# Strided attention on one core: outputs evicted into the place of their Q blocks, and stored four groups at a time

## The chip, the cores and the metric

The kernel runs on one core of one Trainium2 chip. A core has five engines that run their own instruction streams and meet at semaphores: TensorE (PE; its weight loads are listed as PEld), VectorE (DVE), ScalarE (ACT), GpSimd (POOL) and SyncE (SP), which here issues all the transfers. The transfers themselves are done by 16 DMA engines between the chip's memory (HBM) and the on-chip memory SBUF, which has 128 partitions.

The metric is the time of one execution on the device in microseconds (us). The profile is of one such execution, and its span runs from the first to the last instruction.

## The reference

Q, K and V have the shape (8, 12, 1024, 64) in float32. Every query of a head attends to the same 16 key positions, those at multiples of 64:

```python
attend_positions = np.arange(0, seq, stride)          # 0, 64, ..., 960
q = Q[:, :, i:i + 1, :].copy()
k = K[:, :, attend_positions, :].copy()
v = V[:, :, attend_positions, :].copy()
scores = np.einsum('bhqd,bhkd->bhqk', q, k) * scale   # scale = 1 / sqrt(64)
weights = np.exp(scores - np.max(scores, axis=-1, keepdims=True))
weights = weights / (np.sum(weights, axis=-1, keepdims=True) + 1e-10)
result[:, :, i, :] = np.einsum('bhqk,bhkd->bhqd', weights, v)[:, :, 0, :]
```

All of Q is read (96 heads of 256 KiB, 24 MiB), one row in 64 of K and of V (384 KiB each), and an output as large as Q is written.

## The kernel before, in words

The 96 heads are worked on in 24 groups (`NG`) of four heads (`HG`). A group is 1 MiB of Q and 1 MiB of output, 8 KiB in each of the 128 partitions. For group g these steps follow each other:

- `load(g)`: SP issues one transfer of the group's Q into the buffer `qn[g % QBUFS]`. There are 11 such buffers.
- `cast(g)`: POOL copies it to bfloat16 in `qb` (for the first three groups ACT does half).
- `transpose(g)`: DVE transposes it in blocks into `qt`.
- `scores(g)`: PE multiplies by the keys `k_t` into `sc`.
- `largest(g)`, `raise_(g)`, `sums(g)`: DVE takes the maximum and subtracts it, ACT takes the exponential into `ex`, DVE sums and takes the reciprocal.
- `weights(g)`: POOL multiplies `ex` by the reciprocal.
- `turn(g)`, `spread(g)`: PE transposes the weights into `tp`, ACT writes them into `wb`.
- `outputs(g, n)`: PE multiplies by the values `v_all` into the two halves of `o`.
- `evict(g, n)`: ACT copies each half from `o` into an output buffer in SBUF. There are 8 of these (`OBUFS`), in four tiles of two.
- `store(g, n)`: SP issues the transfer of n groups to HBM. Groups 0 to 13 are stored singly, 14 to 21 in pairs, 22 and 23 singly.

The order is written out by hand. Before the main loop K and V are read and spread into `k_t` and, over the first stages, into `v_all` by the small casts of `values`. The main loop goes over stages i; the list `ORDER` names each step with its lag, so that stage i works on the transpose of group i, the cast of i+1, the weights of i-2, the spread of i-3 and the evictions of i-4. Each engine takes its instructions in this order. PE runs a real loop of two stages per turn and counts on "gates", semaphores that the other engines raise; at the end dummy instructions raise them for stages that have no group any more.

SP's queue is ordered by `queue(g)`, the last step of a stage: after the evictions of group g it issues the load of group g+12, if there is one, and then the store, or, for pairs, the store after every second group. The first eleven loads stand in front of the main loop. A load waits for the cast that read its buffer; an eviction into a reused output buffer waits for the store that left it (`after=[stored[g - OBUFS]]`). The very last store is issued after the loop and does not wait for the older ones to land.

`Program.op` records each step with what it reads and writes, and `Program.plan` derives the waits from that; transfers have a "lane" of their own, whose semaphore counts their landing.

Of the kernel before, what the change touches and what calls it, by code (L numbers as in the profile page):

```python
# [168 lines left out]
def kernel(  # L169
# [8 lines left out]
    nc = tc.nc  # L178
# [25 lines left out]
    k_raw = late[:, 0 : NC * D].rearrange("p (n d) -> p n d", d=D)  # L204
    k_half = late[:, NC * D : 2 * NC * D].bitcast(BF16).rearrange("p (a n d) -> p a n d", a=2, d=D)
    k_bf, k_r = [k_half[:, i] for i in range(2)]
# [19 lines left out]

    prog = Program(nc, tc)
    op = prog.op
    stored = {}

    def load(g):
        n = 32
        op("SP", lambda: _copy(
            nc, qn[g % QBUFS],
            _ap_with(Q, [[HG * SD // n, n], [1, HG * SD // n]], g * HG * SD),
        ), writes=[f"qn{g % QBUFS}{h}" for h in range(2)], lane=f"q{g % QBUFS}")

    kv_src = [[stride * D, P], [2 * HG * SD, NC], [1, D]]

    def load_rows(name, tile_, src, lane):  # L240
        op("SP", lambda: nc.sync.dma_start(tile_, _ap_with(src, kv_src)),
           writes=[name], lane=lane)

    load_rows("k_raw", k_raw, K, f"out{OBUFS - 2}")
    load(0)
    load_rows("v_raw", v_raw, V, f"out{OBUFS - 1}")
    for g in range(1, QBUFS):
        load(g)

    op("POOL", lambda: nc.gpsimd.memset(identity, 0.0), writes=["identity"])  # L250
# [11 lines left out]
        op=ALU.max, axis=mybir.AxisListType.XY,  # L262
    ), reads=["identity"], writes=["sel"])
    op("POOL", lambda: nc.gpsimd.memset(v_all, 0.0),  # L264
       writes=[f"v{c}{a}{b}{m}" for c in range(2) for a in range(2) for b in range(2) for m in range(2)] + ["none"])

    def key_rows():
        op("ACT", lambda: nc.scalar.copy(k_bf, k_raw), reads=["k_raw"], writes=["k_bf"])  # L268
# [13 lines left out]
            )[:, h % 2],  # L282
        ), reads=["k_r"], writes=[f"k_t{c}{h}"])

    parts = (slice(0, 2), slice(2, NC))

    apart = []

    def values(c, a, b, m):
        src, dst, part = 32 * (2 * c + b), 32 * (2 * a + b), parts[m]  # L290
        op("POOL", lambda: nc.gpsimd.tensor_copy(  # L291
            out=v_all[dst : dst + 32, 3 + c + 2 * part.start : 3 + c + 2 * part.stop - 1 : 2, 2 * a + b],
            in_=v_raw[src : src + 32, part],
        ), reads=["v_raw"] + apart, writes=[f"v{c}{a}{b}{m}"])
        apart[:] = [f"v{c}{a}{b}{m}"]
# [1 line left out]
    half = 16 * D  # L297

    def cast(g, shared):
        q, b = qn[g % QBUFS], qb[g % 2]  # L300
        if shared:
            op("ACT", lambda: nc.scalar.copy(b[:, half:], q[:, half:]),  # L302
               reads=[f"qn{g % QBUFS}1"], writes=[f"qb{g % 2}1"])
            op("POOL", lambda: nc.gpsimd.tensor_copy(out=b[:, 0:half], in_=q[:, 0:half]),  # L304
               reads=[f"qn{g % QBUFS}0"], writes=[f"qb{g % 2}0"])
        else:
            op("POOL", lambda: nc.gpsimd.tensor_copy(out=b, in_=q),  # L307
               reads=[f"qn{g % QBUFS}{h}" for h in range(2)] + apart,
               writes=[f"qb{g % 2}{h}" for h in range(2)])
            apart[:] = [f"qb{g % 2}0"]  # L310

    def transpose(g):
        k_in = {0: "0", 1: "1"}.get(g)
        words = qt[g % 2].bitcast(I32)
        if g >= NG:
            op("DVE", lambda: nc.vector.memset(qt[g % 2][:, 0:2], 0.0), reads=["low"], writes=[f"qt{g % 2}"],
               gate="turned")
            return
        op("DVE", lambda: nc.vector.transpose(  # L319
            _ap_with(words, [words.ap[0], [1, 2], [D, 16], [2, 32]]), qb[g % 2].bitcast(I32),  # L320
        ), reads=[f"qb{g % 2}0", f"qb{g % 2}1"] + [f"k_t{k_in}{h}" for h in range(4) if k_in],
           writes=[f"qt{g % 2}"], gate="turned")
# [35 lines left out]
           reads=[f"total{g % 2}"], writes=[f"rec{g % 2}"])  # L358

    def weights(g):  # L360
        if g >= NG:
            op("POOL", lambda: nc.gpsimd.memset(wt[g % 2][:, 0:1, 0:2], 0.0), writes=[f"wt{g % 2}"], gate="weighted")
            return
        op("POOL", lambda: nc.gpsimd.tensor_tensor(  # L364
            out=wt[g % 2], in0=ex[g % 2],
            in1=rec[g % 2].unsqueeze(2).to_broadcast([P, 32, NK]), op=ALU.mult,
        ), reads=[f"ex{g % 2}", f"rec{g % 2}"] + [k for k in apart if k[0] == "v"], writes=[f"wt{g % 2}"], gate="weighted")

    def turn_products(g):
        for c in range(4):  # L370
# [29 lines left out]

    def outputs(g, n):
        op("PE", None, reads=[f"wb{g % 2}0", f"wb{g % 2}1"] + [
               f"v{g % 2}{a}{b}{int(g >= 4)}" if 0 <= g < NG else "none" for a in range(2) for b in range(2)
           ], writes=[f"o{n}"], gates=[(f"free{n}", g + 1)] if g >= 0 else [], looped=True)

    def evict(g, n):
        to = out_sb[g % OBUFS].rearrange("p b (c x) d -> p c b (x d)", c=4)
        half = slice(2 * n, 2 * n + 2)
        plain = g >= NG - 1 - 2 * n
        ready = [f"wb{(g + 1) % 2}0", f"wb{(g + 1) % 2}1"] * (n == 0)  # L410
        op("ACT", lambda: nc.scalar.copy(  # L411
            to[:, half], o_ps[:, half].rearrange("p c (b x) -> p c b x", b=2)
        ), reads=[f"o{n}"] + ready, writes=[f"out{g % OBUFS}.{n}"] + ["k_raw", "k_bf", "k_r"] * (g == OBUFS - RUN and not n),
           after=[stored[g - OBUFS]] if g >= OBUFS and not n else [],
           gate=None if plain else f"free{n}", last=g == NG - 1 and n == 1)

        if plain:
            free([f"out{g % OBUFS}.{n}"], n)
# [12 lines left out]
    def store(g, n):  # L431
        both = range(g, g + n)
        sent = op("SP", lambda: send(g, n), lane=f"out{g % OBUFS}",
                  reads=[f"out{i % OBUFS}.{n}" for i in both for n in range(2)])
        stored.update((i, sent) for i in both)

    def idle(i):
        scores(i)
# [24 lines left out]
    quadrants = [[(c, a, b, m) for c in range(2) for a in range(2) for b in range(2)] for m in range(2)]  # L463
    VALUES = {0: quadrants[0]}
    VALUES.update((i + 1, quadrants[1][2 * i : 2 * i + 2]) for i in range(4))

    DEPTH = 4
    turns = (NG + 4) // TURN
    ahead = 1

    def queue(g):
        for n in range(g + QBUFS + ahead if g else QBUFS, g + QBUFS + ahead + 1):
            if n < NG:
                load(n)
        if g < SINGLE or g == NG - 2:
            store(g, 1)
        elif g % RUN == RUN - 1 and g < NG - 1:
            store(g - RUN + 1, RUN)

    def at(i, stage, lag):  # L480
        g = i - lag
        if g in early.get(stage, ()):
            return
        if stage == "transpose" and 0 <= g < NG + 4:
            transpose(g)
        elif stage == "scores" and 0 <= g < NG + 4:
            scores(g)
        elif stage == "weights" and 0 <= g < NG + 2:
# [55 lines left out]
_INS = ['Q', 'K', 'V', 'stride']  # L544
# [31 lines left out]
```

## Time and profile before

| | |
|---|---|
| time, median of 3 runs | 129.38 us (129.22 to 129.51) |
| the profiled execution's own time | 128.91 us |
| its span | 126.7 us |
| busy: PE, DVE, ACT, POOL | 67.0, 86.4, 96.8, 81.8 us |
| moved by DMA | 51.16 MB, mean 404 GB/s |
| read from HBM, written to HBM | 25.95 MB, 25.17 MB |
| loads of Q | 24 of 1 MiB, median 15.6 us from issue to landing |
| stores | 16 of 1 MiB (14.4 us), 4 of 2 MiB (13.4 us) |

How to read the rows that follow: in a timeline a row has the start (us from the span's start), the duration, the engine, the line of the kernel, the operation and the tiles (output, then what it is made from), how many instructions were merged, and in brackets how long the engine had been idle and what ended that. "SPq" is SP's queue, where a row is the issue of a transfer and not the transfer. A row of DMA issues has what is moved, how many issues, KB of each and the median us from issue to landing. A row of the groups has line, engine, operation, shapes and count, then the sum of busy us, the mean ns of one, and the idle time before. A row of waits has who waited for whom, and us in total, times, longest. A row of the table of stretches has from:to, its length, the busy us and the number of instructions of PE, PEld, DVE, ACT and POOL, the granted clock of PE, the mean share of the DMA engines in use, and GB/s.

### The profile page before, as it was taken

Reading aid. Unit: us, or ns where it says so; the run is one execution under the profiler, and the core shown is the slowest. Engines: PE = TensorE matmul, PEld = TensorE weight load, DVE = VectorE, ACT = ScalarE, POOL = GpSimd, SP = SyncE. Lnnn points to the kernel's source line nnn. Section 1 sums busy time; section 2 is a strip of 40 time slices with the busy share of each in tenths; the row PEclk is TensorE's granted clock in tenths of the full one; section 3 lists DMA queues with packets and bytes.
Section 4 is the critical chain, followed back from the end, with each engine's and each line's share of the span. In section 5 each row is a group of like instructions: output and inputs, shape, how many; then the busy total and the mean of one; then the engine's idle time right before and its main releaser. Section 6 shows DMA issues by size and latency. Waiting matters only on the chain. (4 is left out here: it accounts for less than half of the span.)

```text
span 126.7 us, 2269 instructions
## 1 busy us (share of the span) xinstructions
PE 67.0 (53%) x784; PEld 48.7 (38%) x784; DVE 86.4 (68%) x129; ACT 96.8 (76%) x133; POOL 81.8 (65%) x73
## 2 busy tenths in 40 slices
PE   0003893055862666665885466474666658867000
PEld 0003571044642454443664344253554436635000
DVE  3614989565967789999999999999999955200000
ACT  4289614137977999999999999999999999996000
POOL 5982388999999977778877777887777123300000
PEclk9999999955599968998569999999689985699955
DMA  1997998989979899999999899899899999999980
GB/s 46 406 445 341 486 455 372 496 383 445 476 305 522 339 432 440 411 437 445 398 442 463 372 465 476 346 502 406 380 416 429 432 419 445 424 429 419 406 357 39
DMA packets 7141, 51.16 MB, mean 404 GB/s; under 512 B 3808, under 2 KB 3808, under 8 KB 3808
## 3 DMA queue, kind: packets, MB, share of 16 engines
q1 hardware_dynamic: 7136, 51.12, 96.5%
q14 instruction: 5, 0.04, 0.1%
HBM read 25.95 MB, written 25.17 MB: 403 GB/s over the span
## 5 line engine op out<-in xcount | busy, mean ns | idle before, releaser
L411 ACT COPY out_sb<-o 128x1024 f32<-128x1024 f32 x48 | 46.3, 1015 | 2.1
L307 POOL CAST qb<-qn 128x2048 bf16<-128x2048 f32 x21 | 39.7, 1889 | 0.1
L391 PE MATMUL o<-v_all,wb_all 128*128 x224 | 38.4, 313 | 2.2 <-ACTq L421 0.7
L364 POOL TENSOR_TENSOR wt_all<-ex,rec 128x512 bf16<-128x512 f32 x24 | 25.4, 1057 | 21.3 <-DVE rec L357 20.7
L383 ACT ACTIVATE wb_all<-tp,sel 128x512 bf16<-128x512 bf16 x48 | 30.4, 690 | 6.3 <-PE tp L371 6.2
L319 DVE STREAM_TRANSPOSE qt<-qb 128x1024 int32<-128x1024 int32 x24 | 29.8, 1240 | 6.3 <-ACT qb L302 3.3
L327 PE MATMUL sc<-k_t,qt 128*128 x448 | 23.4, 209 | 18.7 <-DVE qt L319 13.6
L327 PEld LDWEIGHTS sc<-k_t,qt 128*128 128x128 bf16 x448 | 20.1, 109 | 25.1 <-issue 23.3
L371 PE MATMUL tp<-identity,wt_all 128*128 128x128 bf16 x112 | 12.9, 249 | 29.0 <-POOL wt_all L364 28.5
L391 PEld LDWEIGHTS o<-v_all,wb_all 128*128 128x128 bf16 x224 | 22.6, 113 | 10.8 <-ACT out_sb L411 4.9
L354 DVE TENSOR_REDUCE total<-ex 128x32 f32<-128x512 f32 x24 | 16.3, 680 | 9.7 <-ACT ex L349 9.7
L349 ACT ACTIVATE ex<-low 128x512 f32<-128x512 f32 x24 | 15.4, 641 | 6.2 <-DVE low L344 6.2
L371 PEld LDWEIGHTS tp<-identity,wt_all 128*128 128x128 bf16 x112 | 7.5, 108 | 32.0 <-POOL wt_all L364 31.3
L344 DVE TENSOR_TENSOR low<-sc,top 128x512 f32<-128x512 f32 x24 | 16.6, 692 | 0.8
L341 DVE TENSOR_REDUCE top<-sc 128x32 f32<-128x512 f32 x24 | 15.2, 632 | 1.3 <-PE sc L327 1.3
L357 DVE RECIPROCAL rec<-total 128x32 f32<-128x32 f32 x24 | 8.5, 353 | 0.8
L291 POOL CAST v_all<-v_raw 32x128 bf16<-32x128 f32 (+1 forms) x16 | 8.0, 500 | 1.0
L264 POOL MEMSET v_all<- 128x7168 bf16 x1 | 6.1, 6071 | 0.0
L304 POOL CAST qb<-qn 128x1024 bf16<-128x1024 f32 x3 | 3.1, 1040 | 4.2 <-DMA qn<-in_Q_dram 4.2
L278 ACT COPY k_t<-out_sb 32x384 bf16<-32x384 bf16 x8 | 4.1, 508 | 0.7 <-DVE out_sb L269 0.6
L302 ACT CAST qb<-qn 128x1024 bf16<-128x1024 f32 x3 | 3.1, 1040 | 0.0
L268 ACT CAST out_sb<-out_sb 128x768 bf16<-128x768 f32 x1 | 0.8, 831 | 2.7 <-DMA out_sb<-in_K_dram 2.7
(14 smaller groups left out, 6.4 us busy)
## 6 DMA issues: line engine op xcount, KB each, us to landing
qn<-in_Q_dram SPq DMA_DIRECT2D x24, 1024.0 KB, 15.6
out_dram<-out_sb SPq DMA_DIRECT2D x16, 1024.0 KB, 14.4
out_dram<-out_sb SPq DMA_DIRECT2D x4, 2048.0 KB, 13.4
out_sb<-in_K_dram SPq DMA_DIRECT2D x1, 384.0 KB, 4.4
v_raw<-in_V_dram SPq DMA_DIRECT2D x1, 384.0 KB, 7.1
```

The source lines that it names most:

```text
L307: op("POOL", lambda: nc.gpsimd.tensor_copy(out=b, in_=q), reads=[f"qn{g % QBUFS}{h}" for h in range(2)] + apart, writes=[f"qb{g % 2}{h}" f ...
L319: op("DVE", lambda: nc.vector.transpose(_ap_with(words, [words.ap[0], [1, 2], [D, 16], [2, 32]]), qb[g % 2].bitcast(I32),), reads=[f"qb{g ...
L327: r = nc.tensor.matmul(sc_ps[g % 2][:, 64 * i : 64 * i + 64], lhsT=_ap_with(qt[g % 2], [qt[g % 2].ap[0], [2, P]], extra_offset=2 * P * i + f),
L341: op("DVE", lambda: nc.vector.tensor_reduce(out=m, in_=s, op=ALU.max, axis=mybir.AxisListType.X,), reads=[f"sc{g % 2}"], writes=[f"top{g % ...
L344: op("DVE", lambda: nc.vector.tensor_tensor(out=low, in0=s, in1=m.unsqueeze(2).to_broadcast([P, 32, NK]), op=ALU.subtract,), reads=[f"sc{g ...
L349: op("ACT", lambda: nc.scalar.activation(out=ex[g % 2], in_=low, func=AF.Exp, bias=0.0, scale=scale,), reads=["low"], writes=[f"ex{g % 2}"])
L354: op("DVE", lambda: nc.vector.tensor_reduce(out=total[g % 2], in_=ex[g % 2], op=ALU.add, axis=mybir.AxisListType.X,), reads=[f"ex{g % 2}"] ...
L364: op("POOL", lambda: nc.gpsimd.tensor_tensor(out=wt[g % 2], in0=ex[g % 2], in1=rec[g % 2].unsqueeze(2).to_broadcast([P, 32, NK]), op=ALU.mult,
L371: r = nc.tensor.transpose(tp_ps[g % 2][:, 2 * c : 2 * c + 2].rearrange("p a b -> p (a b)"), wt[g % 2][:, 8 * c : 8 * c + 8].rearrange("p t ...
L383: op("ACT", lambda a=a: nc.scalar.activation(out=wb[g % 2][:, :, 64 * a : 64 * a + 64], in_=tp_ps[g % 2], func=AF.Copy, scale=sel[:, a : a ...
L391: r = nc.tensor.matmul(_ap_with(o_ps, [o_ps.ap[0], [128, 2], [256, 2], [1, D]], extra_offset=512 * c + D * u,), lhsT=wb[g % 2][:, 2 * c + ...
L411: op("ACT", lambda: nc.scalar.copy(to[:, half], o_ps[:, half].rearrange("p c (b x) -> p c b x", b=2)), reads=[f"o{n}"] + ready, writes=[f" ...
```

## The change

Outputs get no buffers of their own any more. There are 16 buffers in four tiles of four (`quads`, `BUFS`, `RUN`), and each is first the place of a group's Q and then of the same group's output: `evict(g, n)` writes into `qn[g % BUFS]`, whose Q the cast has read long before. K's tiles, which lay in the last output tile, become tiles of their own.

Sixteen loads are issued ahead instead of eleven. A store takes one whole tile: four groups, 4 MiB, rows of 32 KiB per partition, each made of eight pieces of 4 KiB that go to eight places 512 KiB apart in HBM. There are six stores instead of twenty. The eight loads that are left are issued in two batches of four: 16 to 19 right behind the store of groups 4 to 7, when the store of 0 to 3 has landed, and 20 to 23 behind the store of groups 8 to 11, when that of 4 to 7 has landed. The last store, of groups 20 to 23, is the one issued after the loop.

Beside that, the values of the odd groups are cast in one piece each instead of two (`parts[1]`), so that there are 12 casts instead of 16; two of the four dummy steps of `transpose` go, and both dummy steps of `weights`, with the gates raised by several counts at once (`times`).

```diff
-    QBUFS = 11
-    OBUFS = 8
-    RUN = 2
-    SINGLE = 14
+    BUFS = 16
+    RUN = 4
...
-    qn = [sb.tile([P, 32 * D], FP32, name=f"qn{i}") for i in range(QBUFS)]
-    out_all = [sb.tile([P, RUN, 2, 16, D], FP32, name=f"out_sb{i}") for i in range(OBUFS // RUN)]
-    out_sb = [out_all[i // RUN][:, i % RUN] for i in range(OBUFS)]
-    late = out_all[-1].rearrange("p n b x d -> p (n b x d)")
...
+    quads = [sb.tile([P, RUN, 32 * D], FP32, name=f"quad{i}") for i in range(BUFS // RUN)]
+    qn = [quads[i // RUN][:, i % RUN] for i in range(BUFS)]
+    k_raw = sb.tile([P, NC, D], FP32, name="k_raw")
+    k_bf, k_r = [sb.tile([P, NC, D], BF16, name=f"k_half{i}") for i in range(2)]
...
-    for g in range(1, QBUFS):
+    for g in range(1, BUFS):
         load(g)
...
-    parts = (slice(0, 2), slice(2, NC))
+    parts = ((slice(0, 2), slice(2, NC)), (slice(0, NC),))
...
-        ), reads=[f"o{n}"] + ready, writes=[f"out{g % OBUFS}.{n}"] + ["k_raw", "k_bf", "k_r"] * (g == OBUFS - RUN and not n),
-           after=[stored[g - OBUFS]] if g >= OBUFS and not n else [],
+        ), reads=[f"o{n}"] + ready, writes=[f"qn{g % BUFS}{n}"],
            gate=None if plain else f"free{n}", last=g == NG - 1 and n == 1)
...
-    def send(g, n):
-        o = out_sb[g % OBUFS]
+    def send(g):
+        o = quads[g % BUFS // RUN]
         return _copy(
             nc,
-            _ap_with(out, [[16 * D, P], [2 * SD, 2 * n], [1, 16 * D]], g * HG * SD),
-            _ap_with(o, [o.ap[0], [1, 1], [1, 32 * n * D]]),
+            _ap_with(out, [[16 * D, P], [2 * SD, 2 * RUN], [1, 16 * D]], g * HG * SD),
+            _ap_with(o, [o.ap[0], [1, 1], [1, 32 * RUN * D]]),
         )
...
-    VALUES = {0: quadrants[0]}
-    VALUES.update((i + 1, quadrants[1][2 * i : 2 * i + 2]) for i in range(4))
+    VALUES = {0: quadrants[0], 1: quadrants[1][:2], 2: quadrants[1][2:], 3: quadrants[2][:2], 4: quadrants[2][2:]}
...
     def queue(g):
-        for n in range(g + QBUFS + ahead if g else QBUFS, g + QBUFS + ahead + 1):
-            if n < NG:
-                load(n)
-        if g < SINGLE or g == NG - 2:
-            store(g, 1)
-        elif g % RUN == RUN - 1 and g < NG - 1:
-            store(g - RUN + 1, RUN)
+        if g % RUN < RUN - 1 or g == NG - 1:
+            return
+        turn_ = g // RUN
+        store(g - RUN + 1)
+        if 1 <= turn_ <= NG // RUN - BUFS // RUN:
+            first = BUFS + (turn_ - 1) * RUN
+            for n in range(first, first + RUN):
+                load(n)
...
-    end = send(NG - 1, 1)
+    end = send(NG - RUN)
```

More of the change, by code (lines that the diff above doesn't have):

```diff
@@ L190 @@
     assert B * H == NG * HG and S == 1024 and D == 64 and NK == 16 and NG % TURN == 0
-    QBUFS = 11
-    OBUFS = 8
-    RUN = 2
-    SINGLE = 14
+    BUFS = 16
+    RUN = 4
+    assert NG % RUN == 0 and BUFS % RUN == 0
     sb = ctx.enter_context(tc.tile_pool(name="sb", bufs=1))
@@ L228 @@
     op = prog.op
-    stored = {}
     def load(g):
@@ L233, in load @@
         op("SP", lambda: _copy(
-            nc, qn[g % QBUFS],
+            nc, qn[g % BUFS],
             _ap_with(Q, [[HG * SD // n, n], [1, HG * SD // n]], g * HG * SD),
-        ), writes=[f"qn{g % QBUFS}{h}" for h in range(2)], lane=f"q{g % QBUFS}")
+        ), writes=[f"qn{g % BUFS}{h}" for h in range(2)], lane=f"q{g % BUFS}")
     kv_src = [[stride * D, P], [2 * HG * SD, NC], [1, D]]
     def load_rows(name, tile_, src, lane):
-        op("SP", lambda: nc.sync.dma_start(tile_, _ap_with(src, kv_src)),
-           writes=[name], lane=lane)
-    load_rows("k_raw", k_raw, K, f"out{OBUFS - 2}")
+        op("SP", lambda: _copy(
+            nc, tile_, _ap_with(src, kv_src),
+        ), writes=[name], lane=lane)
+    load_rows("k_raw", k_raw, K, "k")
     load(0)
-    load_rows("v_raw", v_raw, V, f"out{OBUFS - 1}")
-    for g in range(1, QBUFS):
+    load_rows("v_raw", v_raw, V, "v")
+    for g in range(1, BUFS):
         load(g)
@@ L264 @@
     op("POOL", lambda: nc.gpsimd.memset(v_all, 0.0),
-       writes=[f"v{c}{a}{b}{m}" for c in range(2) for a in range(2) for b in range(2) for m in range(2)] + ["none"])
+       writes=[f"v{c}{a}{b}{m}" for c in range(2) for a in range(2) for b in range(2) for m in range(2 - c)] + ["none"])
     def key_rows():
@@ L283, in keys @@
         ), reads=["k_r"], writes=[f"k_t{c}{h}"])
-    parts = (slice(0, 2), slice(2, NC))
+    parts = ((slice(0, 2), slice(2, NC)), (slice(0, NC),))
     apart = []
     def values(c, a, b, m):
-        src, dst, part = 32 * (2 * c + b), 32 * (2 * a + b), parts[m]
+        src, dst, part = 32 * (2 * c + b), 32 * (2 * a + b), parts[c][m]
         op("POOL", lambda: nc.gpsimd.tensor_copy(
@@ L299, in cast @@
     def cast(g, shared):
-        q, b = qn[g % QBUFS], qb[g % 2]
+        q, b = qn[g % BUFS], qb[g % 2]
         if shared:
             op("ACT", lambda: nc.scalar.copy(b[:, half:], q[:, half:]),
-               reads=[f"qn{g % QBUFS}1"], writes=[f"qb{g % 2}1"])
+               reads=[f"qn{g % BUFS}1"], writes=[f"qb{g % 2}1"])
             op("POOL", lambda: nc.gpsimd.tensor_copy(out=b[:, 0:half], in_=q[:, 0:half]),
-               reads=[f"qn{g % QBUFS}0"], writes=[f"qb{g % 2}0"])
+               reads=[f"qn{g % BUFS}0"], writes=[f"qb{g % 2}0"])
         else:
             op("POOL", lambda: nc.gpsimd.tensor_copy(out=b, in_=q),
-               reads=[f"qn{g % QBUFS}{h}" for h in range(2)] + apart,
+               reads=[f"qn{g % BUFS}{h}" for h in range(2)] + apart,
                writes=[f"qb{g % 2}{h}" for h in range(2)])
@@ L315, in transpose @@
         if g >= NG:
-            op("DVE", lambda: nc.vector.memset(qt[g % 2][:, 0:2], 0.0), reads=["low"], writes=[f"qt{g % 2}"],
-               gate="turned")
+            op("DVE", lambda: nc.vector.memset(edge[:, g - NG : g - NG + 1], 0.0), gate="turned", times=1 if g == NG else 3)
             return
@@ L366, in weights @@
             in1=rec[g % 2].unsqueeze(2).to_broadcast([P, 32, NK]), op=ALU.mult,
-        ), reads=[f"ex{g % 2}", f"rec{g % 2}"] + [k for k in apart if k[0] == "v"], writes=[f"wt{g % 2}"], gate="weighted")
+        ), reads=[f"ex{g % 2}", f"rec{g % 2}"] + [k for k in apart if k[0] == "v"], writes=[f"wt{g % 2}"], gate="weighted", times=1 if g < NG - 1 else 3)
     def turn_products(g):
@@ L402, in outputs @@
         op("PE", None, reads=[f"wb{g % 2}0", f"wb{g % 2}1"] + [
-               f"v{g % 2}{a}{b}{int(g >= 4)}" if 0 <= g < NG else "none" for a in range(2) for b in range(2)
+               f"v{g % 2}{a}{b}{int(g >= 4 and not g % 2)}" if 0 <= g < NG else "none" for a in range(2) for b in range(2)
            ], writes=[f"o{n}"], gates=[(f"free{n}", g + 1)] if g >= 0 else [], looped=True)
     def evict(g, n):
-        to = out_sb[g % OBUFS].rearrange("p b (c x) d -> p c b (x d)", c=4)
+        to = qn[g % BUFS].rearrange("p (b c x d) -> p c b (x d)", b=2, c=4, d=D)
         half = slice(2 * n, 2 * n + 2)
@@ L412, in evict, with store @@
             to[:, half], o_ps[:, half].rearrange("p c (b x) -> p c b x", b=2)
-        ), reads=[f"o{n}"] + ready, writes=[f"out{g % OBUFS}.{n}"] + ["k_raw", "k_bf", "k_r"] * (g == OBUFS - RUN and not n),
-           after=[stored[g - OBUFS]] if g >= OBUFS and not n else [],
+        ), reads=[f"o{n}"] + ready, writes=[f"qn{g % BUFS}{n}"],
            gate=None if plain else f"free{n}", last=g == NG - 1 and n == 1)
         if plain:
-            free([f"out{g % OBUFS}.{n}"], n)
+            free([f"qn{g % BUFS}{n}"], n)
     def free(reads, n):
         op("ACT", lambda: nc.scalar.nop(), reads=reads, gate=f"free{n}")
-    def send(g, n):
-        o = out_sb[g % OBUFS]
+    def send(g):
+        o = quads[g % BUFS // RUN]
         return _copy(
             nc,
-            _ap_with(out, [[16 * D, P], [2 * SD, 2 * n], [1, 16 * D]], g * HG * SD),
-            _ap_with(o, [o.ap[0], [1, 1], [1, 32 * n * D]]),
-        )
[L431 to L435, printed above, removed]
+            _ap_with(out, [[16 * D, P], [2 * SD, 2 * RUN], [1, 16 * D]], g * HG * SD),
+            _ap_with(o, [o.ap[0], [1, 1], [1, 32 * RUN * D]]),
+        )
+    def store(g):
+        op("SP", lambda: send(g), lane=f"out{g % BUFS // RUN}",
+           reads=[f"qn{i % BUFS}{h}" for i in range(g, g + RUN) for h in range(2)])
     def idle(i):
@@ L462 @@
     )
[L463 to L467 removed]
+    quadrants = [[(c, a, b, m) for a in range(2) for b in range(2)] for c, m in ((0, 0), (1, 0), (0, 1))]
+    VALUES = {0: quadrants[0], 1: quadrants[1][:2], 2: quadrants[1][2:], 3: quadrants[2][:2], 4: quadrants[2][2:]}
     turns = (NG + 4) // TURN
[L469 removed]
     def queue(g):
[L472 to L473 removed]
+        if g % RUN < RUN - 1 or g == NG - 1:
[5 more added lines that the diff above has]
+            for n in range(first, first + RUN):
                 load(n)
[L475 to L478 removed]
     def at(i, stage, lag):
@@ L483, in at @@
             return
-        if stage == "transpose" and 0 <= g < NG + 4:
+        if stage == "transpose" and 0 <= g < NG + 2:
             transpose(g)
@@ L487, in at @@
             scores(g)
-        elif stage == "weights" and 0 <= g < NG + 2:
+        elif stage == "weights" and 0 <= g < NG:
             weights(g)
```

6 lines of the change are left out of this document (removed).

## The prediction

> **What bounds the kernel now.** I read the page first: the lines of sums, the 40 slices and the queues.
>
> ```profile
> span 126.7 us, 2269 instructions
> DMA  1997998989979899999999899899899999999980
> q1 hardware_dynamic: 7136, 51.12, 96.5%
> ```
>
> The DMA engines are busy in every slice but the first and the last, 96.5% of the span, with 51.12 MB on one queue, so transfers set the time over the whole span. The second view is the table of stretches, which shows what the engines do beside that.
>
> ```profile
> 15.00:35.70 20.70, 10.74 (x128) 8.54 (x128) 14.96 (x22) 10.47 (x15) 18.48 (x23) 0.75 1.01 431
> 48.00:109.00 61.00, 39.99 (x471) 28.26 (x468) 54.01 (x84) 59.67 (x84) 41.93 (x31) 0.86 1.01 428
> 124.00:125.00 1.00, 0.00 (x0) 0.00 (x0) 0.00 (x0) 0.00 (x0) 0.00 (x0) 0.50 0.18 74
> 125.00:126.70 1.70, 0.00 (x0) 0.00 (x0) 0.00 (x0) 0.00 (x0) 0.00 (x0) 0.50 0.01 5
> ```
>
> Busy times stand in the order PE, PEld, DVE, ACT, POOL. From 15 to 35.7 us loads flow almost alone, at 431 GB/s: one load of 1 MiB takes 1048.6 KB / 431 = 2.43 us. From 48 to 109 us ACT is busy 59.67 of 61 us. So there are two nearly equal bounds, and computing has no spare speed: a delay in it there is not caught up. The third view is the SP queue's timeline, row by row.
>
> ```profile
> 13.19 0.47 SPq L34 DMA_DIRECT2D qn<-in_Q_dram  x1
> 59.49 0.59 SPq L34 DMA_DIRECT2D out_dram<-out_sb  x1
> 74.24 0.59 SPq L34 DMA_DIRECT2D out_dram<-out_sb  x1
> 88.98 0.54 SPq L34 DMA_DIRECT2D out_dram<-out_sb  x1
> 96.36 0.54 SPq L34 DMA_DIRECT2D out_dram<-out_sb  x1
> 103.73 0.54 SPq L34 DMA_DIRECT2D out_dram<-out_sb  x1
> 110.57 0.54 SPq L34 DMA_DIRECT2D out_dram<-out_sb  x1
> 117.38 0.54 SPq L34 DMA_DIRECT2D out_dram<-out_sb  x1
> ```
>
> A store is issued just after its group's evictions: 59.49 is group 7, 74.24 group 11, 88.98 group 15, 103.73 group 19, 117.38 group 23. Four groups take 14.74 us, one 3.69. The view of DMA issues, asked for one issue at a time, gives the time from issue to landing: here of the load at 13.19 and the stores at 88.98, 96.36, 103.73, 110.57 and 117.38, in this order.
>
> ```profile
> qn<-in_Q_dram SPq DMA_DIRECT2D x1, 1024.0 KB, 25.4
> out_dram<-out_sb SPq DMA_DIRECT2D x1, 2048.0 KB, 17.0
> out_dram<-out_sb SPq DMA_DIRECT2D x1, 2048.0 KB, 14.6
> out_dram<-out_sb SPq DMA_DIRECT2D x1, 2048.0 KB, 12.3
> out_dram<-out_sb SPq DMA_DIRECT2D x1, 2048.0 KB, 10.4
> out_dram<-out_sb SPq DMA_DIRECT2D x1, 1024.0 KB, 8.6
> ```
>
> The double stores land at 105.98, 110.96, 116.03 and 120.97: 5.00 us apart, though issued 7.4 us apart. They queue, and land in the order of issue. The last single store lands at 125.98, two single ones after 120.97, so 2.5 us each. The span ends 0.72 us after that landing. Computing is done at 117.4, but a backlog of 8.6 us is left: the store of the last group is covered by older ones.
>
> **The change, part by part.** Each sum is made against this execution (128.91 us, span 126.7); the median of the runs, 129.38, lies 0.47 us higher, and I add the difference to it.
>
> (1) Start. The values of the odd groups are now cast whole (`parts`, `VALUES`): twelve casts instead of sixteen.
>
> ```profile
> 17.23 1.89 POOL L307 CAST qb<-qn 128x2048 bf16<-128x2048 f32 x1
> 19.18 2.74 POOL L291 CAST v_all<-v_raw 32x128 bf16<-32x128 f32 x8
> 21.98 1.89 POOL L307 CAST qb<-qn 128x2048 bf16<-128x2048 f32 x1
> L291 POOL CAST v_all<-v_raw 32x640 bf16<-32x640 f32 x8 | 5.7, 714 | 0.5
> L291 POOL CAST v_all<-v_raw 32x128 bf16<-32x128 f32 x8 | 2.3, 287 | 0.5
> DVE qt L319 <- POOL qb L307: 3.0, 3, 1.3
> ```
>
> POOL runs without a gap here and DVE waits three times for its Q casts, so POOL is on the path. Four of eight small casts go from the first stage: half of 2.74, 1.37 us. In the next two stages two casts each grow from 640 to 768 elements; by the two sizes an element costs (714-287)/512 = 0.83 ns, so four casts grow by 0.43 us. Gain 0.94 us on all that computing does later; bounds 0 (another engine is next) and 1.37.
>
> (2) Loads and the first store. Sixteen loads go out at once instead of eleven. The load issued at 13.19 is the thirteenth and lands at 38.6; three more end at 45.9. The store of groups 0 to 3 is ready at about 44 (59.49 less four groups and 0.94) and goes straight behind them; it lands at about 55.9. Up to here nothing is lost. Storing four groups at a time holds the outputs of groups 4 to 6 back until group 7 is evicted, at 59.49-0.94 = 58.55, and the queue is empty from 55.9: some 4 us of DMA that the kernel before used.
>
> (3) Loads 16 to 19 now stand in SP's program behind the store of groups 4 to 7, loads 20 to 23 behind that of 8 to 11. By the rows above transfers land in order, so load 16 waits for 4 MiB of store. Four MiB are twice 5.00, 10.0 us. After an empty queue there is a start-up that this trace shows only at its beginning.
>
> ```profile
> 0.00:1.90 1.90, 0.00 (x0) 0.00 (x0) 0.00 (x0) 0.58 (x1) 0.47 (x6) 1.00 0.00 0
> 0.96 0.43 SPq L241 DMA_DIRECT2D out_sb<-in_K_dram  x1
> out_sb<-in_K_dram SPq DMA_DIRECT2D x1, 384.0 KB, 4.4
> ```
>
> The first bytes flow no sooner than 0.9 us after the K issue; at the end bytes stop by 125 and the landing is at 125.98, some 0.5 us or more of finish: at least 1.5. K takes 4.4 us, 0.9 of them for 393 KB at 431 GB/s: at most 3.5. I take the middle, 2.5, as small rows slow K and skew between engines lengthens the rest.
> Load 16 lands at 58.55+2.5+10.0+2.43 = 73.5. The store of 8 to 11 is issued at 73.3 with loads still running, so load 20 follows after three loads, a store and itself: 73.5+7.3+10.0+2.4 = 93.2.
>
> (4) What waits for them.
>
> ```profile
> 69.03 1.89 POOL L307 CAST qb<-qn 128x2048 bf16<-128x2048 f32 x1
> 71.71 1.06 POOL L364 TENSOR_TENSOR wt_all<-ex,rec 128x512 bf16<-128x512 f32 x1 [0.79 <-DVE rec L357]
> 72.82 0.40 PE L371 MATMUL tp<-identity,wt_all 128*128 128x128 bf16 x4 [1.55 <-POOL wt_all L364]
> 72.82 1.25 DVE L319 STREAM_TRANSPOSE qt<-qb 128x1024 int32<-128x1024 int32 x1
> 74.10 1.27 ACT L383 ACTIVATE wb_all<-tp,sel 128x512 bf16<-128x512 bf16 x2
> 83.78 1.89 POOL L307 CAST qb<-qn 128x2048 bf16<-128x2048 f32 x1
> 94.83 1.89 POOL L307 CAST qb<-qn 128x2048 bf16<-128x2048 f32 x1
> ```
>
> The casts at 69.03 and 83.78 are those of groups 16 and 20 (the last, of 23, is at 94.83, and one comes every 3.69 us). Queued behind cast 16 on POOL are the weights of group 13 (71.71), for which the PE transposes and then ACT's spread wait. Slack: cast ends at 70.92, weights 0.79 later; the PE part ends at 73.22, the spread starts 0.88 later. In all 1.67 us (by DVE's transpose 1.90).
> Cast 16 would start at 68.09; its load lands 5.4 later, 3.7 after slack. Cast 20, with that delay, would start at 86.6; its load lands 6.6 later, 5.0 after slack. Computing ends 8.7 us late; loads 17 to 19 and 21 to 23 come every 2.43 us, faster than the 3.69 of a group, and cost nothing.
>
> (5) The end. The last store carries 4 MiB and is issued at 117.38-0.94+8.7 = 125.1. The store before it, ready at about 111.5, has landed by 124, so nothing covers this one: 125.1+2.5+10.0 = 137.6, with 0.72 to the end of the span 138.35. That is 11.65 more: 140.6 for this execution, **141.0** against the median.
>
> (6) Nothing for the rest. Fourteen store issues of 0.54 to 0.59 us go from SP, which waits most of the time; the eviction's wait for an older store goes, and no wait of ACT for DMA is in the trace; the dummy memsets at the end lie beside ACT's last evictions. The separate K tiles change addresses alone.
>
> The rows here bear on two rules of the Trainium skill, DMA: Bandwidth & Descriptors. "Rules for kernel authors" advises merging transfers; its anatomy section puts about 2 us of constant cost on each one. Fourteen fewer stores would be 28 us less by that, an estimate from the page; 5.00 us for 2 MiB beside 2.5 for 1 MiB shows no such constant in a full queue. [...]
>
> **The rivals.**
> A: stores are cheap when merged, 4 MiB taking hardly longer than 1 MiB (the page's constant, above). If x is a store's time, computing is late by max(0, 73.2+2x-84.5) and the end is 116.4+that+2.5+x+0.7. That falls below 126.7 for x under about 6.1 us. At x = 2.5 the span is 122.2, the time about 125. The landings 5.00 apart speak against it. 4%, of which 1% is no change.
> B: loads overtake the store in front of them, so casts are not late. Then the queue's own work decides: from 58.55, 2.5 of start, five stores and eight loads, 69.4, and 0.72: 131.2, a time of 133.9. Against it: landings in order of issue. 7%.
> C: the store's eight pieces per row, each in another head, 512 KiB apart, are slower than two or four. At 11 us a store the end moves by 3 us to 144; at 12, to 147. One and two groups a store cost the same per MiB, which speaks against it. 10%.
> [...] Pieces 512 KiB apart already flow at 428 GB/s here. 2%.
>
> **How the numbers follow.** My forecast has 77%. Its own bounds: start-up 1.5 to 3.5, twice (2 us either way), start gain 0 to 1.37, slack up to 1.9, 4 MiB in 9.8 (428 GB/s) to 10.4. Low ends together give 137.8, high ends 145. With the near part of C inside, 137.5 to 145 leaves out A, B, D and far C, below two in ten. A measurement of this kernel can tell about 0.2%. Only A is faster: 3% faster, 1% same, 96% slower.
>
> **What would show it.** Right: SP has six stores; DMA slices are empty at about 56 to 60; POOL's cast waits for a load of Q twice, 5 to 7 us each; the span's last 12 us hold one store and no engine. Wrong: POOL never waits for Q (B); a store of 4 MiB takes under 7 us (A) or over 11 (C, D) in landings; or the first store comes earlier or later than 44, which moves all the rest.

## The result, and the profile after

The changed kernel takes 141.62 us (median of 4 runs, 141.44 to 142.02) against 129.30 for the kernel before, measured beside it: a ratio of 1.0958, 95% interval 1.0927 to 1.0988. It is 12.3 us slower; 141.0 was forecast, with a range of 137.5 to 145. The profiled execution took 142.02 us, with a span of 140.2.

The lines of the page after that answer to those of before:

```profile
span 140.2 us, 2244 instructions
DMA  1999999999997997098998989999999639773993
q1 hardware_dynamic: 5120, 51.12, 87.9%
```

The same 51.12 MB go through the same queue. Before, the packets took 96.5% of 126.7 us, 122.3 us; now they take 87.9% of 140.2, 123.2 us. So the transfers themselves cost nearly the same, and what they do not fill grew from 4.4 to 17.0 us. The low digits of the DMA line, a slice being 3.5 us, show where it lies. The table of stretches has the places in time (busy us of the engines, then granted clock of PE, DMA share, GB/s):

```profile
55.00:60.00 5.00, 3.02 (x34) 1.90 (x34) 4.49 (x8) 4.91 (x8) 3.75 (x3) 0.89 0.00 0
79.00:82.00 3.00, 3.00 (x30) 2.50 (x29) 2.06 (x4) 2.91 (x5) 3.00 (x3) 0.50 0.71 251
111.00:115.00 4.00, 3.00 (x28) 2.15 (x26) 2.55 (x7) 3.91 (x7) 1.06 (x1) 0.50 0.02 8
125.00:129.00 4.00, 1.94 (x30) 1.25 (x27) 0.00 (x0) 1.54 (x2) 0.00 (x0) 1.00 0.00 0
130.00:139.00 9.00, 0.00 (x0) 0.00 (x0) 0.00 (x0) 0.00 (x0) 0.00 (x0) 0.53 0.95 408
```

The first stretch is the gap while four groups are collected. The third and the fourth are gaps of the same kind ahead of the last two stores, and the fifth is the last store with every engine idle beside it. The second stretch, at 251 GB/s, was not forecast; it comes up again below.

What the gap and the order of the queue did to the engines is in POOL's timeline and the list of waits:

```profile
74.42 1.89 POOL L303 CAST qb<-quad 128x2048 bf16<-128x2048 f32 x1 [5.61 <-DMA quad<-in_Q_dram]
95.62 1.89 POOL L303 CAST qb<-quad 128x2048 bf16<-128x2048 f32 x1 [7.83 <-DMA quad<-in_Q_dram]
POOL qb L303 <- DMA quad<-in_Q_dram: 13.4, 2, 7.8
```

These are the casts of groups 16 and 20, the first of each batch of loads, and no other cast waits in the main loop. SP's timeline and its issues, asked for one by one, give the moments:

```profile
44.41 0.61 SPq L34 DMA_DIRECT2D out_dram<-quad  x1
59.20 0.58 SPq L34 DMA_DIRECT2D out_dram<-quad  x1
59.82 0.60 SPq L34 DMA_DIRECT2D quad<-in_Q_dram  x1
quad<-in_Q_dram SPq DMA_DIRECT2D x1, 1024.0 KB, 14.5
74.62 0.65 SPq L34 DMA_DIRECT2D quad<-in_Q_dram  x1
quad<-in_Q_dram SPq DMA_DIRECT2D x1, 1024.0 KB, 20.9
127.88 0.54 SPq L34 DMA_DIRECT2D out_dram<-quad  x1
out_dram<-quad SPq DMA_DIRECT2D x1, 4096.0 KB, 11.5
```

Load 16, issued at 59.82, lands 14.5 us later, at 74.3, and its cast starts at once. Load 20, issued at 74.62, lands at 95.5. The last store, issued at 127.88, lands at 139.4.

### The profile page after: what moved, and what is told of

It reads as the page before. It is cut to its first block, busy times and chain, and to the rows that moved or that the text cites. A ratio compares the mean times of both kernels' runs of the same rounds, so it can differ in the third digit from the quotient of the medians.

```text
span 140.2 us, 2244 instructions
## 1 busy us (share of the span) xinstructions
PE 71.6 (51%) x784; PEld 54.1 (39%) x784; DVE 86.0 (61%) x127; ACT 97.1 (69%) x133; POOL 81.0 (58%) x67
## 3 DMA queue, kind: packets, MB, share of 16 engines
q1 hardware_dynamic: 5120, 51.12, 87.9%
## 4 chain that ended last, share of the span: by engine, by line
ACT 43%; DMA 18%; POOL 14%; DVE 7%; PE 4%; issue 3%; SPq 0%; ACTq 0%; POOLq 0%; DVEq 0%
ACT quad L403 23%; DMA quad<-in_Q_dram 15%; ACT wb_all L375 13%; POOL qb L303 7%; ACT ex L344 5%; POOL wt_all L356 4%; DMA k_raw<-in_K_dram 4%; DVE qt L314 3%; POOL v_all L287 3%; PE o L383 1%; PE sc L322 1%; ACT k_t L274 1%; DVE total L349 1%; DVE top L336 1%; ACT qb L298 1%
## 5 line engine op out<-in xcount | busy, mean ns | idle before, releaser
L403 ACT COPY quad<-o 128x1024 f32<-128x1024 f32 x48 | 46.3, 1015 | 2.3
L303 POOL CAST qb<-quad 128x2048 bf16<-128x2048 f32 x21 | 39.7, 1892 | 13.5 <-DMA quad<-in_Q_dram 13.4
L383 PE MATMUL o<-v_all,wb_all 128*128 x224 | 42.6, 342 | 2.0 <-ACTq L412 0.7
L314 DVE STREAM_TRANSPOSE qt<-qb 128x1024 int32<-128x1024 int32 x24 | 29.7, 1238 | 14.8 <-POOL qb L303 11.5
L363 PE MATMUL tp<-identity,wt_all 128*128 128x128 bf16 x112 | 14.3, 268 | 37.3 <-POOL wt_all L356 37.3
L322 PE MATMUL sc<-k_t,qt 128*128 x448 | 24.4, 216 | 16.5 <-DVE qt L314 12.7
L322 PEld LDWEIGHTS sc<-k_t,qt 128*128 128x128 bf16 x448 | 22.2, 114 | 21.5 <-issue 19.4
L383 PEld LDWEIGHTS o<-v_all,wb_all 128*128 128x128 bf16 x224 | 25.1, 123 | 11.5 <-ACT quad L403 3.3
L287 POOL CAST v_all<-v_raw 32x128 bf16<-32x128 f32 (+2 forms) x12 | 7.3, 609 | 0.8
L300 POOL CAST qb<-quad 128x1024 bf16<-128x1024 f32 x3 | 3.1, 1040 | 4.6 <-DMA quad<-in_Q_dram 3.1
L274 ACT COPY k_t<-k_half 32x384 bf16<-32x384 bf16 x8 | 4.1, 508 | 0.7 <-DVE k_half L265 0.6
L298 ACT CAST qb<-quad 128x1024 bf16<-128x1024 f32 x3 | 3.1, 1039 | 0.0
## 6 DMA issues: line engine op xcount, KB each, us to landing
out_dram<-quad SPq DMA_DIRECT2D x6, 4096.0 KB, 12.3
```

What stands on the lines that cost most here:

```text
L303: op("POOL", lambda: nc.gpsimd.tensor_copy(out=b, in_=q), reads=[f"qn{g % BUFS}{h}" for h in range(2)] + apart, writes=[f"qb{g % 2}{h}" fo ...
L314: op("DVE", lambda: nc.vector.transpose(_ap_with(words, [words.ap[0], [1, 2], [D, 16], [2, 32]]), qb[g % 2].bitcast(I32),), reads=[f"qb{g ...
L322: r = nc.tensor.matmul(sc_ps[g % 2][:, 64 * i : 64 * i + 64], lhsT=_ap_with(qt[g % 2], [qt[g % 2].ap[0], [2, P]], extra_offset=2 * P * i + f),
L363: r = nc.tensor.transpose(tp_ps[g % 2][:, 2 * c : 2 * c + 2].rearrange("p a b -> p (a b)"), wt[g % 2][:, 8 * c : 8 * c + 8].rearrange("p t ...
L383: r = nc.tensor.matmul(_ap_with(o_ps, [o_ps.ap[0], [128, 2], [256, 2], [1, D]], extra_offset=512 * c + D * u,), lhsT=wb[g % 2][:, 2 * c + ...
L403: op("ACT", lambda: nc.scalar.copy(to[:, half], o_ps[:, half].rearrange("p c (b x) -> p c b x", b=2)), reads=[f"o{n}"] + ready, writes=[f" ...
```

## The experiments

Twelve runs, each beside the kernel before on the same chip; its medians there lay between 129.06 and 129.24. Times below are medians, and gains are against the changed kernel's 141.62. The runs were made on three chips, so runs from different chips are best compared by their distance from the kernel before beside them. The edits are to the changed kernel and are shown by their main lines; in most of them `send` and `store` take a number of groups n, as they did before, and a store's lane goes by its first buffer.

### The same kernel again

No edit.

> The changed kernel once more, nothing edited. In its first profile the packets of load 19 and the first of the store behind it took about 2 us instead of 1.22 at 78 to 81 us, and load 20 came 1.2 us later for it. Theory (a passing disturbance): no slow patch there; load 20's cast waits some 6.6 us instead of 7.8, and the span is about 139. Rival (it belongs to the program, loads and a store meeting at that place): the same patch, span 140.2.

141.83 us (141.41 and 142.25). The slow stretch is there again, if milder in this profile, and cast 20 waits as long as before (8.2 us), so the theory of a passing disturbance falls:

```profile
79.00:82.00 3.00, 3.00 (x30) 2.50 (x29) 2.06 (x4) 2.91 (x5) 2.93 (x3) 0.50 0.82 317
```

### The last four groups stored one by one

```diff
-        store(g - RUN + 1)                  # after every fourth group
+        if g >= NG - RUN: store(g, 1)       # 20, 21, 22; 23 after the loop
+        elif g % RUN == RUN - 1: store(g - RUN + 1)
```

> The changed kernel with one thing undone: groups 20 to 23 are stored one by one, each after its evictions; the other five stores keep four groups. Theory (the queue is served in order, and what is not covered at the end is the work still queued): the store of 16 to 19, issued at 114, lands at 126; groups 20 to 22 wait behind it and 23 comes last, so four MiB still follow 126, to 136: span 136.8, time 138.2, a gain of 3.4 us out of 141.6. Rival (the size of the last transfer alone is what is exposed): issue at 127.9, 2.7 of start and finish, 2.5 for 1 MiB: span 133.9, time 135.3. The late casts at groups 16 and 20 stay (5.6 and 7.8 us of POOL waiting for Q).

138.66 us (138.42 to 138.95), a gain of 3.0, span 136.7. The theory's 138.2 is near, the rival's 135.3 is not: making the last transfer small uncovers the store before it. POOL's waits are the same, 13.7 us.

### Loads ahead of the stores

```diff
-        store(g - RUN + 1)
         if 1 <= turn_ <= NG // RUN - BUFS // RUN:
             first = BUFS + (turn_ - 1) * RUN
             for n in range(first, first + RUN):
                 load(n)
+        store(g - RUN + 1)
```

> The changed kernel with the two batches of loads issued ahead of the store of the same moment instead of behind it; the sizes stay. Theory (casts 16 and 20 are late since their loads stand behind 4 MiB of store): load 16 lands at about 64 and cast 16 does not wait at all; loads 20 to 23 now wait in SP for the store of groups 4 to 7 to land, at about 82, and cast 20 is late by 2 us after slack. The stores of 8 to 23 then follow each other without a gap from 95 to 135: span 135.5, time 136.9, a gain of 4.7. Rival 1 (the lost 8.7 us of computing are all of it): gain 6.5 or more, time 135 or less. Rival 2 (the loads wait for something else than the store in front): POOL still waits 5 us at cast 16 and the time stays within 1 us of 141.6.

136.07 us (135.92 to 136.54), a gain of 5.6. Of the two long waits of POOL one is gone and the other shrinks to 2.0 us, nearly all of it within the slack (the theory had 2 us beyond it):

```profile
POOL qb L303 <- DMA quad<-in_Q_dram: 2.0, 1, 2.0
```

So the casts were late for the store in front of their loads. The time lies under the 136.9 of the theory by 0.8 and does not reach the rival's 135. What is left is the DMA queue's own work after its gaps: from 95 to 133 us it flows at 414 GB/s without a break, and the last store is covered again:

```profile
95.00:133.00 38.00, 14.37 (x176) 9.77 (x174) 9.85 (x18) 20.10 (x27) 5.59 (x5) 0.78 0.97 414
```

### Both

The order of the run before this, and groups 16 to 23 stored one by one.

> Loads ahead of the stores as in the run before, and groups 16 to 23 stored one by one. Theory (after the gaps the queue is full to the end, so its work decides and not the size of the last store): no gain over loads first alone beyond 0.7 us, time 136 to 137. Rival (the last store's 4 MiB are exposed by themselves): 7 us less than loads first alone, time about 130.

136.16 us (135.90 to 136.54): no gain over loads first, as the theory has it. The medians lie 0.1 us apart with the last 8 MiB in eight stores instead of two, so here it does not matter how they are cut.

### The first eight groups stored one by one

```diff
+        if g < 8: store(g, 1)
+        elif g % RUN == RUN - 1: store(g - RUN + 1)     # loads 16 to 23 behind them, as in the change
```

> The changed kernel with groups 0 to 7 stored one by one and the rest in fours; loads 16 to 19 still behind the store of group 7, 20 to 23 behind that of 8 to 11. Theory (the first gap, the DMA engines idle from 56 to 60, and 4 MiB in front of load 16 come from holding groups 4 to 6 back): no gap at 56; load 16 lands at about 68.8 and cast 16 is not late beyond its slack; cast 20 is late by 3.3 us after slack; the last store is still exposed: span 133.8, time 135.3, a gain of 6.3. Rival (the gap is covered by later waiting, only the end counts): time within 1.5 us of 141.6.

136.07 us (135.41 to 136.53), a gain of 5.6 where 6.3 was expected. There is no gap any more from 45 to 65 us; one wait of POOL is 0.3 us, the other, for load 20, is still 6.0, some 1 us more than the theory's 3.3 and the slack:

```profile
45.00:65.00 20.00, 12.66 (x156) 9.14 (x152) 18.62 (x28) 19.48 (x28) 15.89 (x12) 0.84 1.04 439
POOL qb L303 <- DMA quad<-in_Q_dram: 6.3, 2, 6.0
```

### Four transfers for one, first attempt

```diff
-        store(g - RUN + 1)
+        for n in range(g - RUN + 1, g + 1):
+            store(n, 1)
```

> The changed kernel with each store of four groups issued at the same moment as four transfers of 1 MiB: rows of 8 KiB in two pieces, as before, instead of 32 KiB in eight pieces. Only the form of the transfers changes, not when they can start; SP issues three more each time, 0.6 us each, while the first is running. Theory (in a queue a MiB costs the same in either form): time within 0.7 us of 141.6. Rival 1 (eight pieces 512 KiB apart are slower): at 11 us a store instead of 10 three stores on the path make 3 us, so 138.6 or less. Rival 2 (a merged store is cheaper): 143 or more.

135.83 us (135.55 to 135.89), a gain of 5.8, which fits the first rival in size. But the edit did something else than the expectation says. Each of the four transfers waits for its own group only, so SP issues it as soon as that group is evicted: the store of group 4 goes out at 47.6 us and not at 59. The gap at 55 to 60 us is gone for that reason, the same as in the run with the first eight groups stored singly, and the time is that run's. It says nothing on the form of the rows, so the run was made again.

### Four transfers for one, at the same moment

The edit is to the first attempt.

```diff
-           reads=[f"qn{i % BUFS}{h}" for i in range(g, g + n) for h in range(2)])
+        whole = g - g % RUN
+           reads=[f"qn{i % BUFS}{h}" for i in range(whole, whole + RUN) for h in range(2)])
```

> What the run in four transfers was meant to be: each store of four groups as four transfers of 1 MiB, and every one of them waits for the evictions of all four groups, so only the form of the rows differs from the changed kernel (8 KiB in two pieces instead of 32 KiB in eight). In the run before this the four were issued one by one as each group was evicted. Theory (a MiB costs the same in either form; its gain came from the earlier issues): time 141.0 to 142.3, casts 16 and 20 wait 5.5 and 7.5 us again. Rival (the 32 KiB rows cost the time): 136 to 138. Beside that: if load 19 again lands 1.1 us late in front of the store of 8 to 11, the rows of 32 KiB are not the cause of that.

142.13 us (141.69 to 142.49). With the moments kept, rows of 8 KiB in two pieces are no faster than rows of 32 KiB in eight; they are 0.5 us slower, if anything. The waits of POOL are about those of the changed kernel, and so is the slow stretch:

```profile
POOL qb L303 <- DMA quad<-in_Q_dram: 13.5, 2, 8.0
79.00:82.00 3.00, 3.00 (x30) 2.51 (x29) 2.10 (x3) 3.00 (x5) 2.59 (x2) 0.50 0.69 257
```

### K and V issued by the call of before

```diff
-        op("SP", lambda: _copy(nc, tile_, _ap_with(src, kv_src)), ...)
+        op("SP", lambda: nc.sync.dma_start(tile_, _ap_with(src, kv_src)), ...)
```

> The changed kernel with K and V issued as in the kernel before (the other issuing call, 0.43 us for K instead of 0.73). Theory (K landing at 5.0 us after its issue instead of 4.4 is why the start gained only 0.3 us and not 0.94): K lands 0.6 us sooner, all computing is 0.6 us sooner, time 141.0. Rival (K's landing varies by itself, the issue has nothing to do with it): K still takes 5.0, time 141.6.

141.39 us (141.26 to 141.41). K's issue and landing are short again, and the first store goes out at 43.56 instead of 44.41:

```profile
0.96 0.43 SPq L236 DMA_DIRECT2D k_raw<-in_K_dram  x1
k_raw<-in_K_dram SPq DMA_DIRECT2D x1, 384.0 KB, 4.2
43.56 0.63 SPq L34 DMA_DIRECT2D out_dram<-quad  x1
```

The direction holds, and the rival has a share in it. K took 4.2 to 4.4 us to land in the four profiles with this call (that of the kernel before among them) and 4.5 to 5.2 in the ten with the other, so it varies with the same call too. Computing starts 0.85 us sooner than in the first profile of the changed kernel, 0.54 sooner than in its repeated run. The median is 0.2 us less (0.4 against the repeated run), where 0.6 was expected; the intervals of the ratios overlap (1.0916 to 1.0957 here, 1.0927 to 1.0988), so a gain in time is not shown.

### Every group stored by itself, in the shared places

```diff
     def queue(g):
+        if 5 <= g < 5 + NG - BUFS:
+            load(g + BUFS - 5)
+        if g < NG - 1:
+            store(g, 1)
```

> Outputs in the place of their Q blocks, sixteen buffers in four tiles, as in the changed kernel, but every group is stored by itself after its evictions, and load 16+j is issued ahead of the store of group 5+j. Theory (sharing the place costs nothing; the whole loss is the grouping of stores and loads): no late cast, no gap in the DMA engines, the queue full to the end: time 129.0, within 0.7 of the kernel before. Rival (evicting into the Q tiles, or sixteen loads ahead, costs by itself): 131 or more.

129.91 us (129.52 to 130.37), 1.0062 of the kernel before (1.0042 to 1.0083). Of the 12.3 us, 11.7 are gone with the grouping alone. Two casts of the main loop still wait for a load, 2.2 us together, which the theory excluded. What is left was taken apart in the next two runs.

### The same with K and V issued by the call of before

The edits of the two runs before this.

> Shared places and single stores, with K and V issued by the call of the kernel before (K's issue 0.43 us instead of 0.73; the first bytes flow 0.3 us sooner). Theory (the queue is full from its first byte to its last, so a start 0.3 us sooner ends 0.3 us sooner): 129.6, and 0.3 over the kernel before stays for the form of the stores. Rival (K's issue is nothing): 129.9.

129.39 us (128.98 to 130.10), 1.0025 of the kernel before (1.0005 to 1.0044). The two runs stood on different chips; from the kernel before beside them they lie 0.67 and 0.33 us, so the call is worth some 0.3 us, as the theory has it, but the two intervals just touch.

### The stores of before in the shared places

```diff
+        if g < 14 or g == NG - 2: store(g, 1)
+        elif g % 2 and g < NG - 1: store(g - 1, 2)
```

> Shared places, K and V issued by the call of the kernel before, and its schedule of stores: groups 0 to 13 singly, 14 to 21 in pairs, 22 and 23 singly; loads as in the run with single stores. Theory (sharing the place costs nothing by itself): 129.2, within 0.3 of the kernel before. Rival (eviction into Q's tiles or sixteen loads ahead cost something): 129.6 or more. A gain over the kernel before by more than 0.3 is not expected by either, since the queue is full in both.

128.89 us (128.59 to 129.72), 0.9989 of the kernel before (0.9970 to 1.0008): no difference can be told. Eviction into the place of the Q blocks, sixteen loads ahead, the K tiles of their own and the new cuts of the values together cost nothing and bring nothing that can be told. Beside the run before this one, on the same chip, there is a difference: 0.5 us less with twenty stores than with twenty-four, twelve runs each. That is the 0.3 over the kernel before that the expectation of that run kept for the form of the stores, and a little more. The queue is as full as before:

```profile
span 127.2 us, 2263 instructions
q1 hardware_dynamic: 7136, 51.12, 96.1%
```

### Only the later groups in fours

Groups 0 to 7 and the loads as with single stores, groups 8 to 23 in four stores of 4 MiB.

> Groups 0 to 7 singly and the loads ahead of the stores at the pace of the groups, as with single stores; groups 8 to 23 in fours, the last with 4 MiB issued after the loop. Theory (without late casts the queue is nearly worked off when computing ends at 117.4, and the last store of 4 MiB then stands alone): 117.4 + 2.7 + 9.9 and 0.8 to the end, span 130.8, time 133.1; POOL does not wait for Q after the start. Rival (the exposed last store costs the whole 7.4 us of three more MiB): 137.

132.12 us (131.26 to 132.54), 1.0 less than the theory's 133.1 and far from the rival's 137. The cost over single stores is 2.2 us (2.4 when each is taken from the kernel before beside it). The last store stands alone, after a short gap:

```profile
117.00:119.00 2.00, 0.61 (x4) 0.31 (x4) 0.00 (x0) 0.29 (x1) 0.00 (x0) 1.00 0.00 0
119.00:130.00 11.00, 0.00 (x0) 0.00 (x0) 0.00 (x0) 0.00 (x0) 0.00 (x0) 0.64 0.89 381
POOL qb L303 <- DMA quad<-in_Q_dram: 2.8, 1, 2.8
```

POOL does wait once for 2.8 us, which the theory excluded. The span of the profiled execution is the theory's 130.8, but by luck: the last store was issued at 118.5 and not 117.4, and landed 11.5 us later and not 12.6; the other three executions have spans of 129.5 to 130.4.

## Why the prediction was right

The direction, the size and the mechanism were right: POOL waited for a load of Q exactly twice, the queue ran empty at 55 to 60 us, and one store with no engine beside it ended the span. Taken step by step, some errors cancelled, and that the medians agree to 0.6 us is in part luck.

(1) The start. Computing ran only 0.29 us sooner (the store after group 7 was issued at 59.20 against 59.49), not 0.94. The sum itself was good: in the three profiles of the new casts with K issued as before, the eviction of group 3 began at 41.08 to 41.26 against 42.23, 1.0 to 1.15 us sooner. "The separate K tiles change addresses alone" was wrong by an edit beside it, which stands in the whole kernel and not in the diff above: K is issued by another call, took 5.0 us to land instead of 4.4, and all that computing does stands behind it.

(2) The gap. Forecast at some 4 us from 55.9; the engines are empty from 55 to 60.

(3) The loads. Load 16 was forecast for 73.5 and landed at 74.3, of which 0.65 is the missing gain of the start. Load 20 was forecast for 93.2 and landed at 95.5. Part of that is the same 0.65; the rest is that the 8 MiB between the two landings took 21.2 us where 19.7 were forecast, 396 GB/s instead of 426. By an estimate from the table of stretches 0.9 us of it was lost from 73 to 85 us, where the mean was 393 GB/s, the slow stretch included. That is a term the prediction did not have.

(4) What waits for them. Cast 16 was late by 74.42 - (69.03 - 0.29) = 5.7 us (forecast 5.4). The slack of 1.67 can be checked on ACT: the spread behind it came at 78.03 instead of 74.10 - 0.29, a delay of 4.2, so the slack was worth 1.5.

```profile
78.03 1.26 ACT L375 ACTIVATE wb_all<-tp,sel 128x512 bf16<-128x512 bf16 x2 [4.07 <-PE tp L363]
```

Nothing was caught up behind it. Computing ended 10.8 us late (127.88 against 117.38 - 0.29), where 8.7 was forecast.

(5) The end. The last store took 11.5 us and not 12.5: over the 10.0 of a full queue it paid 1.5, the lower bound of the start-up term, and not 2.5. The span ended 0.8 us after that. Together: 125.1 + 12.5 + 0.7 became 127.9 + 11.5 + 0.8; computing was under-forecast by 2.8 (0.65 from the start, most of the rest from load 20), the last store over-forecast by 1.0, and the sum is off by 1.85 in the span. Against the medians it is off by 0.6 only: this execution is 0.4 above its median, the one of before was 0.47 below, and 1.8 us instead of 2.2 lie outside the span.

(6) The transfers. "A MiB costs the same" holds for the form of the rows within some 0.5 us of the whole time (142.13 against 141.62 at the same moments; 136.16 against 136.07 in a full queue), and what difference there is goes against the smaller stores. With that C (eight pieces are slower) falls. A (merged stores are cheap) needed 4 MiB in under about 6 us; the three stores that met an empty queue, issued at 59.20, 114.15 and 127.88, landed 11.5 to 12.7 us later:

```profile
out_dram<-quad SPq DMA_DIRECT2D x1, 4096.0 KB, 12.7
114.15 0.59 SPq L34 DMA_DIRECT2D out_dram<-quad  x1
out_dram<-quad SPq DMA_DIRECT2D x1, 4096.0 KB, 11.8
```

They paid 1.5 to 2.7 us over the 10.0 of a full queue. D, a store at half the rate, has no run that shows it: pieces of 4 KiB that step by 512 KiB within a row flowed at 408 to 419 GB/s.

The merging rule of the Trainium skill, DMA: Bandwidth & Descriptors, section "Rules for kernel authors", which speaks of many small transfers, brought little for stores of 1 MiB and more where the queue was full: four stores fewer were worth 0.5 us together (129.39 against 128.89). The constant of about 2 us in its section "Anatomy of one DMA — SWDGE (gpsimd) path" is given there for transfers issued from GpSimd, and all transfers here are issued by SP; in a full queue the runs show some 0.1 us for a store, and 1.5 to 2.7 in an empty one.

B, loads overtaking the store in front of them, fell already by POOL's waits; and moving the loads in front took most of the waiting away (2.0 us of 13.4 was left).

(7) The range. By the bounds that the prediction names, the low ends together come to 137.5 and not 137.8 (2.0 for the start-ups, 0.43 for the start, 0.6 for three stores, 0.46 for the slack, off 141.0); the range given begins there.

How the 12.3 us divide depends on which part is undone first, since the gaps, the late casts and the last store stand in one queue and cover each other. The early groupings alone, undone, give 5.6; the order of loads alone 5.6; the last store alone 3.0; the late groupings, with all else undone, cost 2.2; all of the grouping 11.7.

No version here beats the kernel before by more than the measurement can tell.

## What to carry to other kernels

When the DMA queue is the bound, a store's price is not its issue but what the queue can do while the store is not yet ready, and who stands behind it: storing four groups at once emptied the queue three times and put 10 us in front of a load that was wanted 5 us earlier. A merged store at the end stands alone behind the computing, 11.5 us here, unless older work is still queued by then; beside single stores, which leave a backlog of their own (8.6 us in the kernel before), it cost 2.2 to 3.0 us. And look at which event each transfer waits for before reading a run as a test of its form: the first attempt at four transfers for one changed their moments, and the gain came from that.

## What was not expected of the hardware

Where a batch of loads was followed by a store that was already queued, the rate fell for some 3 us: 251, 317 and 257 GB/s at 79 to 82 us in the changed kernel, its repetition and the run with four transfers at the same moment, against 437 and 448 on both sides in the first of them. Two more profiles have the same moments, those with the last four groups singly and with K issued by the call of before, and there the same 3 us show 350 and 382. Over the 12 us from 73 to 85 all five agree, 390 to 396 GB/s, and the cast of group 20 waits 7.8 to 8.2 us in each. So the loss belongs to the program and the deep dip does not always; rows of 8 KiB show it as rows of 32 KiB do. It is not far from the usual: the kernel before moved 403 to 448 GB/s in stretches of 12 us between 48 and 96. The cause is open. In the runs where loads and single stores alternate, the whole time comes within 0.7 us of the kernel before, so there it costs little.

The second thing is the call that issues K: the same transfer of 128 x 12 rows of 256 bytes took 0.73 us to issue by one call and 0.43 by the other, and landed 4.5 to 5.2 us after its issue against 4.2 to 4.4. Where the DMA queue is full from end to end that was worth some 0.3 us of the whole time, which is at the edge of what these runs can tell.
